# Moving the start addresses of two activation tiles in a two-layer decoder kernel

## The chip, the cores and the metric

The kernel runs on one core of a Trainium2 chip. The metric is the device time of one execution in microseconds. Three runs of the kernel before gave 1098.22, 1100.28 and 1100.70 us, so its median is 1100.28 us.

## The reference, cut to what matters

Two residual layers over 512 tokens of width 1024, in float32. Every layer is a mixer and then an MLP, each behind an RMS norm:

```
for i in range(2):
    h = rmsnorm(x, norm_mix[i])
    x = x + (mix_even(h, ...) if i % 2 == 0 else mix_odd(h, ...))
    h = rmsnorm(x, norm_mlp[i])
    x = x + mlp(h, w1[i], w2[i])

def mlp(h, w1, w2):              # w1: 1024 x 4096, w2: 4096 x 1024
    a = relu(h @ w1)
    return (a * a) @ w2
```

`mix_even` projects h and runs gated linear attention beside block-sparse softmax attention; `mix_odd` projects h and runs a short gated convolution beside a pooling mixer. Both end in a 1024 x 1024 output projection.

## The kernel before, in words

Activations lie transposed, features on the 128 partitions and the 512 tokens along the free dimension. Every large matrix product is done in three passes of a split type: an operand is kept as a rounded part `hi` and a remainder `lo`, and `mm3` (lines 126 to 129) issues hi x hi, hi x lo and lo x hi into one PSUM accumulation. So each 128 x 128 weight slice costs three matmuls of 512 columns (lines 127, 128, 129), each with its own load of 128 weight columns into TensorE (LDWEIGHTS).

Weights stream in as 184 blocks of 128 x 1024 float32. `block_parts` (lines 100 to 114) issues the DMA of a block into `raw` on SP's queue, ScalarE rounds it into `whi` (line 111) and VectorE subtracts it into `wlo` (line 112); two blocks are prepared ahead. A block feeds 24 matmuls of 512 columns.

The moving operand of these matmuls, the one that streams its columns past the loaded weights, is nearly always the tile `A`: 32 rows of 512 float32, that is 32 x 2048 bytes per partition. Rows 0 to 7 and 8 to 15 hold `hi` and `lo` of the normed layer input, rows 16 to 23 and 24 to 31 those of a mixer's output or of a group of the MLP's inner activations. The token projections (`tok_g`) use it the other way round, with `A` as weights and the weight block as moving operand.

The MLP works on four groups of 1024 inner features: `m1(g)` makes group g, `m2(g)` multiplies it by w2 and adds to x. Groups 0 and 2 lie in rows 16 to 31 of `A`, groups 1 and 3 in the tile `E`, 16 rows of 2048 bytes. The order is m1(0), m1(1), m2(0), m1(2), m2(1), m1(3), m2(2), m2(3), in program order on TensorE. The very last product of the kernel (`last_unit`) does half of its columns in pieces of 256.

Where the tiles lie: a pool's tiles follow each other in each partition in multiples of 32 bytes, and the pools follow each other. `A` is the last tile of pool `cp`; behind it come `wp` (raw, whi, wlo), `np` (norm helpers `ss`, `nt`, `rs`), and then the pools of the stage at hand, among them `E` and, in the odd mixer, `pwh`, `pwl` and `ph`. Before the change `A` starts at byte 40,896 of a partition, `raw` at 106,432, the first `whi` at 114,624, `E` at 155,584. What is left of these starts on division by 256 is the same, 192, and since rows are 2048 bytes and weight slices 512 bytes long, every row of `A` and `E` and every weight slice of `whi` and `wlo` starts on remainder 192 as well. Tiles with another remainder are rare: `ph` (pooling input, moving in lines 127 to 129 under the name pm, with `pwh` and `pwl` at 192 as weights) and `th` (softmax weights, moving in line 690, with `A` at 192 as weights) both start on remainder 0. `ones_r` (192, the weights of the norm sums nps, lines 275 and 276) and `kk` lie ahead of `A`.

Of the kernel before, what the change touches and what calls it, by code (L numbers as in the profile page):

```python
# [8 lines left out]
F32R = mybir.dt.float32r  # L9
# [5 lines left out]
P = 128  # L15
S = 512
# [28 lines left out]
def kernel(  # L45
# [14 lines left out]
    cp = ctx.enter_context(tc.tile_pool(name="cp", bufs=1))  # L60
# [16 lines left out]
    warm = cp.tile([P, 64], F32, name="warm")  # L77
    dve.memset(warm, 0.0)
    kk = cp.tile([P, KT, S], F32R, tag="x", name="kk")
    A = cp.tile([P, 32, S], F32R, name="A")  # L80
    ident = cn[:, C_ID : C_ID + P]
    ones = cn[:, C_ONE : C_ONE + P]
    dist = cn[:, C_DIST : C_DIST + S]
# [4 lines left out]
    def col(i, n=1):  # L88
        return vc[:, i : i + n]

    def mm_tile(name):
        return ps.tile([P, 2, S], F32, tag="mm", name=name, bufs=2)

    def m_tile(name, tag="tp"):
        return ps.tile([P, S], F32, tag=tag, name=name, bufs=2 if tag == "s" else 1)
# [23 lines left out]
    def wblock():  # L119
        while len(ready) < AHEAD + 1 and wcount[0] < w.shape[0]:  # L120
            emit_block()
        return ready.pop(0)

    def mm3(o, w_hi, w_lo, a_hi, a_lo, start, stop, swap=False):
        if swap:
            w_hi, w_lo, a_hi, a_lo = a_hi, a_lo, w_hi, w_lo
        pe.matmul(o, w_hi, a_hi, start=start, stop=False)  # L127
        pe.matmul(o, w_hi, a_lo, start=False, stop=False)  # L128
        pe.matmul(o, w_lo, a_hi, start=False, stop=stop)  # L129

    def t_unit_g(name, acts):
        o = mm_tile(name)
        n = len(acts)
        for b in range(n // 4):
# [3 lines left out]
            for kk in range(4):  # L138
                k = b * 4 + kk
                for j in range(2):  # L140
                    c = slice(j * P, (j + 1) * P)
                    mm3(o[:, j, :], hi[:, kk, c], lo[:, kk, c], A[:, acts[k][0], :], A[:, acts[k][1], :],
                        k == 0, k == n - 1)
# [11 lines left out]
    def t_unit(name, acts):  # L155
        return drain(t_unit_g(name, acts))

    def tok_g(name, evac):
        blocks = []
        for half in range(2):  # L160
            o = mm_tile(f"{name}{half}")
            for k in range(KT):
# [4 lines left out]
                for j in range(2):  # L167
                    t = slice((2 * half + j) * P, (2 * half + j + 1) * P)
                    mm3(o[:, j, :], hi[:, c], lo[:, c], A[:, k, t], A[:, 8 + k, t], k == 0, k == KT - 1, swap=True)
                if k == KT - 1:  # L170
# [84 lines left out]
    def split_h(k, gcol, src, c=slice(0, S)):  # L255
        act.activation(A[:, k, c], src[:, k, c], AF.Copy, scale=col(gcol + k))
        dve.scalar_tensor_tensor(  # L257
            A[:, 8 + k, c], src[:, k, c], col(gcol + k), A[:, k, c].bitcast(F32), op0=ALU.mult, op1=ALU.subtract
        )
# [23 lines left out]
    def bc2(t):  # L283
        return t[:, None, :].to_broadcast([P, 2, S])

    def x_add(o, n):
        dve.tensor_add(x[:, 2 * n : 2 * n + 2, :], x[:, 2 * n : 2 * n + 2, :], o)  # L287
# [13 lines left out]
    def mlp(l, nrm, nxt):  # L301
        with ExitStack() as c2:
            mp = c2.enter_context(tc.tile_pool(name=f"mp{l}", bufs=2, reuse_waits="tile"))
            E = mp.tile([P, 16, S], F32R, tag="E", name=f"E{l}", bufs=1)
            st = {}

            def aslot(f):
                i = f % 8
                if (f // 8) % 2 == 0:
                    return A[:, 16 + i, :], A[:, 24 + i, :]  # L310
                return E[:, i, :], E[:, 8 + i, :]

            def apair(f):
                i = f % 8
                if (f // 8) % 2 == 0:
                    return A[:, 16 + i : 18 + i, :], A[:, 24 + i : 26 + i, :]
                return E[:, i : i + 2, :], E[:, 8 + i : 10 + i, :]

            def m1(g):
                for q in range(4):  # L320
                    f = 8 * g + 2 * q
                    o = t_unit(f"m1_{l}_{f}", H)
                    if "rs" not in st:
                        st["rs"] = nrm.rs()
                    r = mp.tile([P, 2, S], F32, tag="r", name=f"r_{l}_{f}")
                    dve.scalar_tensor_tensor(r, o, 0.0, bc2(st["rs"]), op0=ALU.max, op1=ALU.mult)  # L326
                    act.activation(r, r, AF.Square)  # L327
                    hi, lo = apair(f)
                    act.copy(hi, r)  # L329
                    dve.tensor_sub(lo, r, hi.bitcast(F32))  # L330

            def last_unit(g, n):
                ws = [[t.rearrange("p (k n) -> p k n", k=4) for t in wblock()] for _ in range(2)]
                for j, c0, c1 in ((0, 0, S), (1, 0, S // 2), (1, S // 2, S)):
                    c = slice(j * P, (j + 1) * P)
                    row = 2 * n + j
                    o = m_tile(f"m2_{l}_{g}_{n}_{j}_{c0}", "tp" if c0 else "s")
                    for k in range(8):
                        hi, lo = ws[k // 4]
                        ah, al = aslot(8 * g + k)  # L340
                        mm3(o[:, c0:c1], hi[:, k % 4, c], lo[:, k % 4, c], ah[:, c0:c1], al[:, c0:c1], k == 0, k == 7)
                    dve.tensor_add(x[:, row, c0:c1], x[:, row, c0:c1], o[:, c0:c1])
                    nc.sync.dma_start(out[row * P : (row + 1) * P, c0:c1], x[:, row, c0:c1])

            def m2(g):
                for n in range(4):
                    if nxt is None and g == 3 and n == 3:
                        last_unit(g, n)
                        return
                    o = mm_tile(f"m2_{l}_{g}_{n}")  # L350
                    for b in range(2):
                        hi, lo = wblock()
                        hi = hi.rearrange("p (k n) -> p k n", k=4)
                        lo = lo.rearrange("p (k n) -> p k n", k=4)
                        for kk in range(4):
                            k = 4 * b + kk
                            ah, al = aslot(8 * g + k)
                            for j in range(2):
                                c = slice(j * P, (j + 1) * P)
                                mm3(o[:, j, :], hi[:, kk, c], lo[:, kk, c], ah, al, k == 0, k == 7)  # L360
                    x_add(o, n)
                    if g == 3:
                        for k in (2 * n, 2 * n + 1):
                            if nxt is not None:
                                nxt.step(k)
                            else:
                                nc.sync.dma_start(out[k * P : (k + 1) * P, :], x[:, k, :])

            m1(0)
            m1(1)  # L370
            m2(0)
            m1(2)
            m2(1)
            m1(3)
            m2(2)
            m2(3)
# [547 lines left out]
    even_mixer(n0, n1)  # L924
    n2 = Norm("n2", V_MIX + 8)
    mlp(0, n1, n2)
    n3 = Norm("n3", V_MLP + 8)
    odd_mixer(n2, n3)
    mlp(1, n3, None)


# [122 lines left out]
```

## Time and profile before

| | |
|---|---|
| median of three runs | 1100.28 us |
| profiled execution | 1100.57 us |
| its span, first to last instruction | 1098.8 us |
| PE busy | 1087.6 us, 99% of the span |
| DVE, ACT, POOL busy | 556.4, 405.4, 103.2 us |
| granted TensorE clock, mean | 0.998 |

A matmul's duration in the trace covers its whole passage through the array, and matmuls overlap; what one costs in a stream is the distance from its start to the start of the next, called its gap below.

### The profile page before, as it was taken

Reading aid. Unit: us, or ns where it says so; the run is one execution under the profiler, and the core shown is the slowest. Engines: PE = TensorE matmul, PEld = TensorE weight load, DVE = VectorE, ACT = ScalarE, POOL = GpSimd, SP = SyncE. Lnnn points to the kernel's source line nnn. Section 1 sums busy time; section 2 is a strip of 40 time slices with the busy share of each in tenths; the row PEclk is TensorE's granted clock in tenths of the full one; section 3 lists DMA queues with packets and bytes.
Section 4 is the critical chain, followed back from the end, with each engine's and each line's share of the span. In section 5 each row is a group of like instructions: output and inputs, shape, how many; then the busy total and the mean of one; then the engine's idle time right before and its main releaser. Section 6 shows DMA issues by size and latency. Waiting matters only on the chain.

```text
span 1098.8 us, 12567 instructions
## 1 busy us (share of the span) xinstructions
PE 1087.6 (99%) x5008; PEld 889.5 (81%) x5008; DVE 556.4 (51%) x774; ACT 405.4 (37%) x554; POOL 103.2 (9%) x110
## 2 busy tenths in 40 slices
PE   9999999999999999999999999999999999999998
PEld 6677778778888888888888888888888888888887
DVE  6887766767534334334334675455444344334331
ACT  6465555545434223224214332244433133133110
POOL 2132322314000000000001200021000000000000
PEclk9999999999999999999999999999999999999999
DMA  7223114122332322223322332323232223222231
GB/s 229 77 77 96 58 39 154 42 69 84 115 96 96 96 96 96 95 96 96 96 96 96 106 96 96 96 96 96 96 96 96 96 96 96 96 96 96 96 115 58
DMA packets 32043, 104.84 MB, mean 95 GB/s; under 512 B 3729, under 2 KB 6258, under 8 KB 31986
## 3 DMA queue, kind: packets, MB, share of 16 engines
q1 hardware_dynamic: 31202, 101.69, 28.5%
q0 software_dynamic: 640, 2.10, 0.6%
q8 instruction: 39, 0.64, 0.2%
q10 hardware_dynamic: 144, 0.26, 0.1%
q14 instruction: 18, 0.15, 0.0%
HBM read 101.94 MB, written 2.10 MB: 95 GB/s over the span
## 4 chain that ended last, share of the span: by engine, by line
PE 92%; DVE 4%; ACT 1%; DMA 1%; POOL 1%; issue 1%; SPq 0%; DVEq 0%; POOLq 0%
PE m L129 21%; PE m L128 21%; PE m L127 21%; PE wo L129 1%; PE wo L128 1%; PE wo L127 1%; DMA raw<-in_w_dram 1%; PE av L690 1%; PE s L642 1%; PE ptp L671 1%; PE s L641 1%; PE va L127 1%; PE va L129 1%; PE va L128 1%; PE xc L129 1%
## 5 line engine op out<-in xcount | busy, mean ns | idle before, releaser
L111 ACT CAST whi<-raw 128x1024 fp32r<-128x1024 f32 (+1 forms) x188 | 194.4, 1035 | 537.5 <-PE m L128 432.0
L112 DVE TENSOR_TENSOR wlo<-raw,whi 128x1024 fp32r<-128x1024 f32 (+1 forms) x188 | 228.1, 1214 | 201.4 <-ACT whi L111 201.2
L127 PE MATMUL m<-A,whi 128*128 128x512 f32 x768 | 298.8, 389 | 0.0
L128 PE MATMUL m<-A,whi 128*128 128x512 f32 x768 | 298.8, 389 | 0.0
L129 PE MATMUL m<-A,wlo 128*128 128x512 f32 x768 | 298.8, 389 | 0.0
L128 PEld LDWEIGHTS m<-A,whi 128*128 128x128 f32 x768 | 144.2, 188 | 30.1
L127 PEld LDWEIGHTS m<-A,whi 128*128 128x128 f32 x768 | 144.2, 188 | 29.8
L129 PEld LDWEIGHTS m<-A,wlo 128*128 128x128 f32 x768 | 144.2, 188 | 29.7
L128 PE MATMUL m<-E,whi 128*128 128x512 f32 (+1 forms) x264 | 101.0, 383 | 0.0
L129 PE MATMUL m<-E,wlo 128*128 128x512 f32 (+1 forms) x264 | 101.0, 383 | 0.0
L127 PE MATMUL m<-E,whi 128*128 128x512 f32 (+1 forms) x264 | 101.0, 383 | 0.0
L287 DVE TENSOR_TENSOR x<-x,m 128x1024 f32<-128x1024 f32 x31 | 37.9, 1221 | 109.1 <-PE m L129 109.1
L326 DVE SCALAR_TENSOR_TENSOR r<-m,rs_n 128x1024 f32<-128x1024 f32 x32 | 39.2, 1225 | 96.8 <-PE m L129 96.7
L268 POOL TENSOR_TENSOR ss_n<-ss_n,sq_n 128x512 f32<-128x512 f32 x21 | 32.8, 1562 | 391.7 <-ACT sq_n L266 391.0
L127 PEld LDWEIGHTS m<-E,whi 128*128 128x128 f32 x264 | 49.6, 188 | 9.8
L128 PEld LDWEIGHTS m<-E,whi 128*128 128x128 f32 x264 | 49.6, 188 | 9.7
L129 PEld LDWEIGHTS m<-E,wlo 128*128 128x128 f32 x264 | 49.6, 188 | 9.5
L327 ACT ACTIVATE r<-r 128x1024 f32<-128x1024 f32 x32 | 34.0, 1061 | 19.9 <-DVE r L326 19.9
L330 DVE TENSOR_TENSOR E<-r,E 128x1024 fp32r<-128x1024 f32 x16 | 19.6, 1225 | 17.2 <-ACT E L329 17.2
L257 DVE SCALAR_TENSOR_TENSOR A<-x,vc,A 128x512 fp32r<-128x512 f32 x24 | 27.3, 1141 | 1.2
L330 DVE TENSOR_TENSOR A<-r,A 128x1024 fp32r<-128x1024 f32 x16 | 19.6, 1225 | 15.1 <-ACT A L329 15.1
L127 PE MATMUL wo<-A,whi 128*128 128x512 f32 x64 | 24.9, 389 | 0.0
(297 smaller groups left out, 1414.3 us busy)
## 6 DMA issues: line engine op xcount, KB each, us to landing
raw<-in_w_dram SPq DMA_DIRECT2D x180, 512.0 KB, 3.3
xin<-in_xT_dram SPq DMA_DIRECT2D x16, 128.0 KB, 3.9
raw<-in_w_dram SPq DMA_DIRECT2D x8, 256.0 KB, 4.3
x<-in_xT_dram POOLq DMA_DIRECT2D x8, 256.0 KB, 4.9
out_dram<-x SPq DMA_DIRECT2D x7, 256.0 KB, 2.0
cn<-in_con_dram SPq DMA_DIRECT2D x1, 736.0 KB, 6.7
pw<-in_poolw_dram ACTq DMA_DIRECT2D x1, 256.0 KB, 2.7
out_dram<-x SPq DMA_DIRECT2D x2, 128.0 KB, 1.7
```

Source lines behind the costliest of these rows:

```text
L111: act.copy(hi[:, c], raw[:, c])
L112: dve.tensor_sub(lo[:, c], raw[:, c], hi[:, c].bitcast(F32))
L127: pe.matmul(o, w_hi, a_hi, start=start, stop=False)
L128: pe.matmul(o, w_hi, a_lo, start=False, stop=False)
L129: pe.matmul(o, w_lo, a_hi, start=False, stop=stop)
L257: dve.scalar_tensor_tensor(A[:, 8 + k, c], src[:, k, c], col(gcol + k), A[:, k, c].bitcast(F32), op0=ALU.mult, op1=ALU.subtract)
L268: (dve if first else pool).tensor_add(ss, ss, sq)
L287: dve.tensor_add(x[:, 2 * n : 2 * n + 2, :], x[:, 2 * n : 2 * n + 2, :], o)
L326: dve.scalar_tensor_tensor(r, o, 0.0, bc2(st["rs"]), op0=ALU.max, op1=ALU.mult)
L327: act.activation(r, r, AF.Square)
L330: dve.tensor_sub(lo, r, hi.bitcast(F32))
L641: pe.matmul(s_[:, :m], qs, kS[p][hh][:, :m], start=True, stop=False)
```

## The change

`A` is allocated 64 bytes longer, and the kernel uses it from byte 64 on. As everything behind `A` in the partition follows it, the weight tiles, the norm helpers and all later pools move by 64 bytes too. `E` is allocated 192 bytes longer and is used from byte 128 on in layer 0 and from byte 192 on in layer 1; the tiles behind `E` in its pool (`r`) move by these 192 bytes on top. No instruction is added, removed or reordered.

```diff
-    A = cp.tile([P, 32, S], F32R, name="A")
+    A = cp.tile([P, 32 * S + 16], F32R, name="A")[:, 16:].rearrange("p (k s) -> p k s", s=S)
...
-            E = mp.tile([P, 16, S], F32R, tag="E", name=f"E{l}", bufs=1)
+            e0 = (32, 48)[l]
+            E = mp.tile([P, 16 * S + 48], F32R, tag="E", name=f"E{l}", bufs=1)[:, e0 : e0 + 16 * S]
+            E = E.rearrange("p (k s) -> p k s", s=S)
```

Remainders of the starts on division by 256 bytes:

| tile | before | after |
|---|---|---|
| `A` | 192 | 0 |
| `whi`, `wlo`, `raw` | 192 | 0 |
| `E`, layer 0 / layer 1 | 192 / 192 | 128 / 192 |
| norm helpers `nt` | 192 | 0 |
| `ones_r`, `kk` | 192 | 192 |
| `ph` with `pwh` as weights | 0 with 192 | 64 with 0 |
| `th` with `A` as weights | 0 with 192 | 64 with 0 |

## Rows read from the trace of the kernel before

**Rows 1.** The page: span, part 1, the clock of part 2, part 4.

```profile
span 1098.8 us, 12567 instructions
PE 1087.6 (99%) x5008; PEld 889.5 (81%) x5008; DVE 556.4 (51%) x774; ACT 405.4 (37%) x554; POOL 103.2 (9%) x110
PEclk9999999999999999999999999999999999999999
PE 92%; DVE 4%; ACT 1%; DMA 1%; POOL 1%; issue 1%; SPq 0%; DVEq 0%; POOLq 0%
```

**Rows 2.** Instruction groups by shape, PE: line, names, tile, count | busy us, mean ns.

```profile
L127 PE MATMUL m<-A,whi 128*128 128x512 f32 x768 | 298.8, 389 | 0.0
...
L127 PE MATMUL m<-E,whi 128*128 128x512 f32 x248 | 96.5, 389 | 0.0
```

**Rows 3.** Timeline of PE (start us, us), two rows 192 matmuls apart, moving operand A.

```profile
318.59 0.39 PE L127 MATMUL m<-A,whi 128*128 128x512 f32 x1
...
362.11 0.39 PE L127 MATMUL m<-A,whi 128*128 128x512 f32 x1
```

**Rows 4.** Timeline of PE, the 192 matmuls on E of m2(1), layer 0.

```profile
438.27 0.39 PE L127 MATMUL m<-E,whi 128*128 128x512 f32 x1
...
481.79 0.39 PE L127 MATMUL m<-A,whi 128*128 128x512 f32 x1
```

**Rows 5.** Stretches: us, busy by engine, then PEclk (granted clock), DMA, GB/s.

```profile
33.00:34.80 1.80, 1.80 (x5) 1.36 (x5) 1.01 (x7) 0.52 (x2) 0.00 (x0) 0.50 0.81 198
276.00:317.00 41.00, 41.00 (x182) 33.97 (x181) 20.99 (x19) 16.47 (x17) 0.00 (x0) 1.00 0.30 97
```

**Rows 6.** Timeline of PE in the first of these stretches.

```profile
33.14 0.63 PE L127 MATMUL kb<-whi,A 128*128 128x512 f32 x1
...
33.99 0.63 PE L129 MATMUL kb<-whi,A 128*128 128x512 f32 x1
```

**Rows 7.** Timeline of PE around pm, whose moving operand starts on another remainder.

```profile
645.44 0.40 PE L127 MATMUL pm<-ph,pwh 128*128 128x512 f32 x1
645.68 0.40 PE L128 MATMUL pm<-ph,pwh 128*128 128x512 f32 x1
...
646.83 0.40 PE L127 MATMUL xc<-A,whi 128*128 128x512 f32 x1
...
649.15 0.39 PE L128 MATMUL xc<-A,whi 128*128 128x512 f32 x1
```

**Rows 8.** Timeline of PE around the norm sums nps.

```profile
274.62 0.39 PE L275 MATMUL nps_n<-ss_n,ones_r 128*128 128x512 f32 x1
274.85 0.39 PE L276 MATMUL nps_n<-ss_n,ones_r 128*128 128x512 f32 x1
...
275.98 0.39 PE L128 MATMUL m<-A,whi 128*128 128x512 f32 x1
```

**Rows 9.** Matmuls of 256 columns by line: duration ns min/median/max, first and last start.

```profile
L127 PE MATMUL m<-E,whi x12: 283/283/283, 1090.5 to 1094.5; 128*128 128x256 f32 x12
...
L690 PE MATMUL av<-th,A x3: 278/279/280, 145.7 to 145.9; 128*128 128x256 f32 x3
```

**Rows 10.** Timeline of PE, 46 gaps of 256 columns on E.

```profile
1089.53 0.28 PE L128 MATMUL m<-E,whi 128*128 128x256 f32 x1
...
1095.05 0.28 PE L129 MATMUL m<-E,wlo 128*128 128x256 f32 x1
```

**Rows 11.** VectorE by line, 1024 elements, operands on different remainders: ns min/median/max.

```profile
L326 DVE SCALAR_TENSOR_TENSOR r<-m,rs_n x32: 1224/1225/1225, 279.1 to 1008.0; 128x1024 f32<-128x1024 f32 x32
...
L899 DVE TENSOR_TENSOR cg<-cg,rs x2: 1223/1224/1225, 645.6 to 679.7; 128x1024 f32<-128x1024 f32 x2
```

**Rows 12.** Waits: who for whom, us in total, times, longest.

```profile
ACT whi L111 <- PE m L128: 432.0, 119, 4.4
...
ACT whi L111 <- DMA raw<-in_w_dram: 12.0, 9, 4.3
```

## The prediction

> **What bounds the kernel now.** I read the page first. PE is busy 99% of a span of 1098.8 us at a granted clock whose mean is 0.9 or more in each of the 40 slices, and the chain that ended last lies on PE for 92% of the span [rows 1]. So time is decided by the gap from one matmul's start to the next, and by little else. Next the groups by shape: on each of the lines 127 to 129, 768 matmuls of 512 columns stream rows of A and 248 stream rows of E in the MLPs, all with a mean duration of 389 ns and no idle time before them [rows 2]. Durations overlap, so I went to the timeline. 192 matmuls on A take 362.11 - 318.59 = 43.52 us, a gap of 226.7 ns [rows 3]; 192 on E take 481.79 - 438.27 = 43.52 us, the same gap [rows 4].
>
> Is 226.7 ns the least that 512 columns can cost? The early stretch says no. At a granted clock of 0.50, the lower level of 1.2 GHz, against 1.00 later on [rows 5], two gaps take 33.99 - 33.14 = 0.85 us, 425 ns each, which is one column per cycle (512/1.2 = 426.7) with nothing on top [rows 6]. One column per cycle at 2.4 GHz would be 213.3 ns. At full clock each matmul therefore pays 13.3 ns, or 32 cycles, that it doesn't pay at half the clock. A fixed cost per instruction would not vanish at the lower clock; two streams of reads that get in each other's way at the full rate could. The two streams would be the moving row and the weight slice of the next matmul, which is loaded beside it. The 256-column matmuls on E agree: 46 gaps take 1095.05 - 1089.53 = 5.52 us, 120.0 ns each, and 256/2.4 = 106.7, so again 13.3 ns more [rows 10]. In all these rows both streams start on the same remainder modulo 256 bytes.
>
> Do remainders matter at all? Two places let me look. pm streams `ph` (remainder 0) against weights at 192. The regular gap ends with its first matmul: 0.24 us to the second [rows 7]. From pm's start to the xc matmul at 649.15 there are 16 gaps in 3.71 us, 231.9 ns each; only then is the gap 226.7 again. nps is a change of tiles too, with weights and moving both at 192, and its gaps stay regular: from 274.62 to 275.98 six gaps take 1.36 us, 226.7 ns each [rows 8]. So a difference of remainders between moving and weights disturbs the stream, not a change of tile. The second place is av, `th` at 0 against weights at 192: its 256-column matmuls last 278 to 280 ns where those on E last 283 [rows 9]. Duration less gap is 389 - 227 = 162 for 512 columns [rows 2, 3] and 283 - 120 = 163 for 256, so av's gaps are some 3 to 5 ns shorter than E's.
>
> **The change, part by part.** No instruction is added, removed or moved, no semaphore or queue changes.
>
> 1. A and all behind it move by 64 bytes. The 184 blocks x 24 matmuls are 4,416; less the 744 on E (3 x 248) and less 24 that the last product replaces by 48 of 256 columns, 3,648 stream A against weights or weights against A. Both sides move alike, so the difference of remainders stays 0. I cost this at nothing. Nothing in the trace shows all tiles moved together, so the bounds are 5.2 ns to either side (the 231.9 of [rows 7] less 226.7), 19 us each way; I keep that as a rival, since the nearest row, a stream with equal remainders, keeps its gap whichever row or slice is used [rows 3, 4].
>
> 2. E against its weights: the difference becomes 128 bytes in layer 0 and 192 in layer 1, for 744 matmuls of 512 columns and 48 of 256. Not shown before, so bounded by rows. Below: no interference, 213.3 ns, so 744 x 13.3 = 9.9 us less, and 48 x 13.3 = 0.6 us less. Above: the unsettled stream of pm and xc, 744 x 5.2 = 3.9 us more, and 0.2 us more for the 48. Of the two rows with a difference, pm's is six matmuls after a break and runs on into xc, where the difference is 0 again, so it shows the break and not what an unequal stream settles at; av is the one that recurs with its own gap, and it is 3 to 5 ns shorter. I take 5 ns a matmul, above a third of the 13.3: 744 x 5 + 48 x 3 = 3.9 us less.
>
> 3. Breaks. E starts and ends four times, and each passage may cost what pm's did: 3.71 - 16 x 0.2267 = 0.08 us. Eight times is 0.6 us at most; as pm's 0.08 holds two breaks (into pm, out of it), 0.3 us. nps now has a difference (192 for `ones_r`, 0 for `nt`) in the three places that are in steady stream: 0.2 us. Together 0.5 us more. The attention matmuls that mix A with `kk`, 32 of them, could move by 13 ns at most, 0.4 us either way; I count none.
>
> 4. VectorE, ScalarE, the DMAs. A 1024-element operation takes 1225 ns on tiles at 192 and 1224 on `cg`, which starts on remainder 0 [rows 11], so their prices stay. What hides them: ScalarE waits 432.0 us in total for TensorE before it rounds the next weights, and 12.0 us for the DMA [rows 12]. If PE gains 4 us over the four stretches on E, some 180 us long, this cover, up to 4.4 us a block, is still there, and nothing else comes late.
>
> Sum: 0 - 3.9 + 0.5 = 3.4 us less than the profiled execution's 1100.57 us (its span and 1.8 us around it), 1097.2 us. That execution is 0.3 us over the median, so against the median 1096.9; I say 1097.0.
>
> The Trainium skill puts a bare figure on the gap: "TensorE: Matmul & The Clock Gate", section "Back-to-back issue gap", gives N/2.4 + 2.5 ns for a warm isolated one, 215.8 ns for 512 columns. By it, E freed of all interference would give an estimated 744 x 10.9 = 8.1 us, and the time would be about 1093; the trace before shows no 512-column gap that short in a steady stream.
>
> **Rivals.**
>
> (a) E settles at the old gap. A disturbed stream finds its way back to 226.7 (as xc does 10 matmuls after pm), whatever the difference. For it: the two lengths, 512 and 256 columns, pay exactly the same 13.3 ns; against it: av. Then only the breaks are left: 1100.6 + 0.5, against the median 1100.8 us.
> The Trainium skill speaks for this one: "SBUF — State Buffer", section "A bandwidth-pool intuition that's wrong", gives LDWEIGHTS a second, independent read port, so the streams could not meet and no address would matter; the irregular gaps behind pm speak against a rule that strict.
>
> (b) Slower: E never settles. The regular gap is a state that needs equal remainders, and E's 744 matmuls run like the 16 of pm and xc. Its place is the four stretches on E, its price 3.9 + 0.2 us, with the breaks 4.6 us more: 1104.9 us. It decides from a gap of 226.7 on: every ns above it is 0.74 us. For it: pm shows nothing settling in six matmuls; against it: xc was just as irregular with equal remainders, and av is regular and shorter.
>
> (c) The start itself counts, not the difference: with A and the weights on remainder 0 all 3,648 matmuls change. At 5.2 ns that is 19 us: 1081 or 1119. Against it: pm's moving operand starts on 0 and is not quicker for it.
>
> (d) The addresses don't move as the diff says, because the space behind A is laid out anew; then E alone would differ, and the time is that of the forecast, (a) or (b).
>
> **How the numbers follow.** Forecast 0.44, reaching from 1090 (nothing left of the 13.3 ns, breaks added) to 1099 (2 ns gained); (a) 0.29, 1100 to 1101.5; (b) 0.20, 1102 to 1105; (c) 0.07, of which 0.04 down and 0.03 up; (d) is spread over the others. Range for 8 in 10: 1090 to 1105; that leaves out (c) and the edges of the forecast and of (b). What a measurement of this kernel can tell from no change is about 0.2%, 2.2 us: below 1098.1 faster, above 1102.5 slower. Faster: 0.42 of the forecast's 0.44 and 0.04 of (c), 0.46. Slower: 0.19 of (b) and 0.03 of (c), 0.22. The rest, 0.32, is the same.
>
> **What would show it.** Step 1: 192 matmuls on A still take 43.52 us. Step 2: the 192 on E take 42.6 us (gap 221.7); 43.5 would be rival (a), 44.5 rival (b). Layer 0 and layer 1 need not agree, since 128 and 192 bytes differ. Step 3: irregular gaps for some ten matmuls behind each change between A and E and behind nps. Step 4: the same durations on VectorE and ScalarE, and ScalarE still waiting for TensorE and not for the DMA. The prediction is wrong at its root if the gap on A moves.

## The result: slower, 1106.57 us for 1099.59

Four runs each: 1106.57 us (1105.02 to 1107.53) with the change, 1099.59 us (1098.22 to 1100.70) before, a ratio of 1.0063 with a 95% interval of [1.0045, 1.0081]. The profiled execution took 1107.12 us, 6.55 more than that of before.

The page of the kernel after, the lines that answer to [rows 1]: the span, the busy times, the clock in 40 slices, the chain.

```profile
span 1105.3 us, 12567 instructions
PE 1093.2 (99%) x5008; PEld 890.8 (81%) x5008; DVE 556.2 (50%) x774; ACT 405.5 (37%) x554; POOL 102.6 (9%) x110
PEclk9899999999999999999999999999999999999999
PE 92%; DVE 3%; ACT 1%; DMA 1%; POOL 1%; issue 1%; SPq 0%; POOLq 0%; DVEq 0%
```

The same instructions, the same engines busy for the same time, except PE. So to the timeline of PE after: a stretch of 192 matmuls on A, answering [rows 3], then m2(1) on E in layer 0, answering [rows 4], and m2(1) on E in layer 1 (start us, us).

```profile
320.36 0.39 PE L127 MATMUL m<-A,whi 128*128 128x512 f32 x1
...
363.88 0.39 PE L127 MATMUL m<-A,whi 128*128 128x512 f32 x1
...
440.04 0.40 PE L127 MATMUL m<-E,whi 128*128 128x512 f32 x1
...
484.83 0.39 PE L127 MATMUL m<-A,whi 128*128 128x512 f32 x1
...
925.17 0.39 PE L127 MATMUL m<-E,whi 128*128 128x512 f32 x1
...
969.97 0.39 PE L127 MATMUL m<-A,whi 128*128 128x512 f32 x1
```

A: 363.88 - 320.36 = 43.52 us, as before, a gap of 226.7 ns. E: 44.79 and 44.80 us, gaps of 233.3 ns, 6.7 ns or 16 cycles longer, in both layers; in layer 1 every gap lies between 232 and 235 ns, in layer 0 they alternate between some 229 and 238 about the same mean. The other two E stretches do the same (44.79 us for 192 and 39.20 for 168; before 43.52 and 38.08). Together the four lost 4.9 us.

One thing on E became faster. The 256-column matmuls at the very end, which answer [rows 10]:

```profile
1096.35 0.28 PE L128 MATMUL m<-E,whi 128*128 128x256 f32 x1
...
1101.57 0.28 PE L129 MATMUL m<-E,wlo 128*128 128x256 f32 x1
```

46 gaps in 5.22 us, 113.5 ns each, where before they took 120.0: 0.3 us won. VectorE and the wait for the DMA are as they were; these rows answer to [rows 11, 12] (duration min/median/max, and waits).

```profile
L328 DVE SCALAR_TENSOR_TENSOR r<-m,rs_n x32: 1223/1225/1225, 280.8 to 1013.7; 128x1024 f32<-128x1024 f32 x32
...
L901 DVE TENSOR_TENSOR cg<-cg,rs x2: 1223/1224/1224, 650.0 to 684.1; 128x1024 f32<-128x1024 f32 x2
```

```profile
ACT whi L111 <- PE m L128: 436.5, 119, 4.6
...
ACT whi L111 <- DMA raw<-in_w_dram: 12.2, 9, 4.3
```

That makes 4.9 - 0.3, and some 0.1 for the breaks (a stretch on A behind an E stretch or behind nps takes 43.53 to 43.54 us instead of 43.52). The rest of the 6.55 us arises ahead of E: its first matmul starts at 440.04 us after and at 438.27 before. Whether these 1.8 us belong to the change is the first thing to ask.

### The profile page after: what moved, and what is told of

Its sections match the earlier page's. It is cut to its first block, busy times and chain, and to the rows that moved or that the text cites. A ratio compares the mean times of both kernels' runs of the same rounds, so it can differ in the third digit from the quotient of the medians.

```text
span 1105.3 us, 12567 instructions
## 1 busy us (share of the span) xinstructions
PE 1093.2 (99%) x5008; PEld 890.8 (81%) x5008; DVE 556.2 (50%) x774; ACT 405.5 (37%) x554; POOL 102.6 (9%) x110
## 4 chain that ended last, share of the span: by engine, by line
PE 92%; DVE 3%; ACT 1%; DMA 1%; POOL 1%; issue 1%; SPq 0%; POOLq 0%; DVEq 0%
PE m L128 21%; PE m L129 21%; PE m L127 21%; PE wo L129 1%; PE wo L127 1%; PE wo L128 1%; PE av L692 1%; DMA raw<-in_w_dram 1%; PE s L644 1%; PE ptp L673 1%; PE s L643 1%; PE va L127 1%; PE va L129 1%; PE va L128 1%; PE xc L127 1%
## 5 line engine op out<-in xcount | busy, mean ns | idle before, releaser
L127 PE MATMUL m<-E,whi 128*128 128x512 f32 (+1 forms) x264 | 102.4, 388 | 0.0
L128 PE MATMUL m<-E,whi 128*128 128x512 f32 (+1 forms) x264 | 102.3, 388 | 0.0
L328 DVE SCALAR_TENSOR_TENSOR r<-m,rs_n 128x1024 f32<-128x1024 f32 x32 | 39.2, 1224 | 96.9 <-PE m L129 96.8
L332 DVE TENSOR_TENSOR A<-r,A 128x1024 fp32r<-128x1024 f32 x16 | 19.6, 1224 | 15.1 <-ACT A L331 15.1
```

## The experiments

Theory D: what counts is the difference between the start of the moving row and the start of the weight slice, modulo 256 bytes. Its rivals: the start itself (S), and a cost in the first 60 us (C).

**Each part alone.** `a_alone` has the first hunk of the diff only, `e_alone` the second only.

```diff
 a_alone
+    A = cp.tile([P, 32 * S + 16], F32R, name="A")[:, 16:].rearrange("p (k s) -> p k s", s=S)
 e_alone
+            e0 = (32, 48)[l]
+            E = mp.tile([P, 16 * S + 48], F32R, tag="E", name=f"E{l}", bufs=1)[:, e0 : e0 + 16 * S]
```

> The first part of the change alone: A, the weight tiles and all behind them 64 bytes later, E on the same remainder as the weights again. Theory D (the gap is set by the difference of the starts of moving row and weight slice modulo 256 bytes; equal starts 226.7 ns, those of E in the change 233.3): every E stretch of 192 matmuls back to 43.5 us, all of A at 43.5 us, so the time of before within 0.2%, plus whatever the first 62 us add. Theory S (the start itself counts, or anything that moves with the 64 bytes): the time goes up by part of the 6.5 us here, most of it outside E. Theory C (1.6 us of the change's 6.5 us lie in the first 60 us and come from the 64 bytes): about 1.6 us slower than before, all of it before 62 us.

> The second part alone: E 128 and 192 bytes later in the two layers, A and the weights where they were. Theory D: the same differences as in the change, so each E stretch takes 44.8 us and the time rises by about 5.1 us (4 x 1.27), 0.46%. Theory S: E now starts on remainder 64 in layer 0 and 128 in layer 1, other starts than in the change; the stretches need not take 44.8 us, and layer 0 and layer 1 would change places at best. Theory C: none of the 1.6 us in the first 62 us.

`a_alone`: 1100.49 us against 1100.09, ratio 1.000 [0.9989, 1.0012]. `e_alone`: 1105.10 us, ratio 1.0042 [1.0026, 1.0058]. Timeline of `a_alone`, m2(1) of layer 0:

```profile
438.51 0.39 PE L127 MATMUL m<-E,whi 128*128 128x512 f32 x1
...
482.03 0.39 PE L127 MATMUL m<-A,whi 128*128 128x512 f32 x1
```

and of `e_alone`, m2(1) of both layers:

```profile
439.37 0.40 PE L127 MATMUL m<-E,whi 128*128 128x512 f32 x1
...
484.16 0.39 PE L127 MATMUL m<-A,whi 128*128 128x512 f32 x1
...
924.45 0.39 PE L127 MATMUL m<-E,whi 128*128 128x512 f32 x1
...
969.25 0.39 PE L127 MATMUL m<-A,whi 128*128 128x512 f32 x1
```

43.52 us where all moved together; 44.79 and 44.80 where E moved against the weights, the very times of the change, though E now starts on remainders 64 and 128 instead of 128 and 192. The differences, 128 and 192, are what the two kernels share. S falls. C falls too: E's first matmul comes at 438.51 us in `a_alone`, with the 64 bytes, and at 439.37 in `e_alone`, without them.

**The change once more**, unaltered, in six runs.

> The change once more, unaltered, for a tighter ratio. Theory D (only E's difference to the weights costs): 4 stretches x 1.27 us, so 0.46%, like E moved alone (0.42% measured); the 1.6 us that the change's first profile lost before 62 us were chance and are not there in the median. If the two parts add something together: over 0.6% again, and A's stretches or the first 62 us show where.

1105.31 us against 1100.43, ratio 1.0051 [1.0033, 1.0068]. Its first matmul on E starts at 437.8 us, earlier than before's; in the other runs of this study that leave A at its gap, that start lies anywhere from 435.9 to 439.5. So the 1.8 us of the first profile don't belong to the change. They go with the clock that TensorE was granted: here are the stretches from 20 to 40 us of the kernel before and of the first profile after (us, busy by engine, granted clock, DMA, GB/s).

```profile
20.00:40.00 20.00, 17.96 (x79) 12.50 (x78) 15.99 (x32) 10.76 (x19) 4.20 (x4) 0.91 0.41 130
...
20.00:40.00 20.00, 16.90 (x69) 11.91 (x69) 13.57 (x28) 9.27 (x18) 3.67 (x4) 0.83 0.40 132
```

0.91 before and 0.83 after; 0.08 of 20 us is 1.6 us. The mean granted clock of a whole run varies from 0.997 to 1.0 over the runs, and the time goes with it (the kernel before: 1102.6 us at 0.997, 1098.9 at 1.0, medians); why it varies the runs don't show. At one and the same mean clock, 0.998, the change took 1105.11 us (median of 5 runs) and the kernel before 1100.45 (of 14): 4.7 us. What the traces account for, 4.9 - 0.3 + 0.1 = 4.7 us or 0.43%, is just that; it lies inside this run's interval and that of E alone, and just under the first one's lower end of 0.45%.

**The weights moved instead.** In `w_moved` A stays and all behind it goes 64 bytes later.

```diff
+    A = cp.tile([P, 32 * S + 16], F32R, name="A")[:, : 32 * S].rearrange("p (k s) -> p k s", s=S)
```

> A stays where it was and the weight tiles, with E and all else behind A, go 64 bytes later: E's difference to the weights is 0 again, A's becomes 192 (64 in the token projections, where A is the weights). Theory D, with the weights as the partner: every A stretch of 192 goes from 43.5 to 44.8 us, E's stay at 43.5; 3,264 matmuls x 6.67 ns and 384 x 2.3 ns make 22.7 us, about 1122 us. If the partner were anything else (A's other rows, the stores of the other engines into E): A's stretches stay at 43.5 us and the time at 1100 us.

1120.81 us against 1100.43, ratio 1.0189 [1.0171, 1.0207]; 20.4 us more by the medians where 22.7 were expected. Timeline of `w_moved`: a stretch on A, and m2(1) on E.

```profile
319.41 0.40 PE L127 MATMUL m<-A,whi 128*128 128x512 f32 x1
...
364.21 0.40 PE L127 MATMUL m<-A,whi 128*128 128x512 f32 x1
...
442.61 0.39 PE L127 MATMUL m<-E,whi 128*128 128x512 f32 x1
...
486.17 0.39 PE L127 MATMUL m<-A,whi 128*128 128x512 f32 x1
```

Now A, which did not move, takes 44.80 us, and E, which moved with the weights, 43.56 (0.04 of it a break). The partner of the moving row lies behind A, and the weights are what TensorE reads there. What is missing of the 22.7 us lies ahead of the first MLP: from its first matmul on the span grew by 19.2 us, just what the 2,880 matmuls on A that stand there cost at 6.67 ns each. The stores of other engines and of the DMA into the moved tiles are a rival, but in m2(1) of layer 1 after the change, where every gap is long, VectorE and ScalarE work in only 15.55 and 10.43 of 44.70 us and the DMA engines in 30% of it, so their stores don't explain it (the view of [rows 5]):

```profile
925.20:969.90 44.70, 44.70 (x193) 35.90 (x192) 15.55 (x13) 10.43 (x10) 0.00 (x0) 1.00 0.30 95
```

**The differences, four to a run.** E got an offset of its own in m2(1) and m2(3) of each layer.

```diff
+            EO = ((16, 24), (40, 56))[l]
+            Et = mp.tile([P, 16 * S + 56], F32R, tag="E", name=f"E{l}", bufs=1)
+            Eg = [Et[:, e : e + 16 * S].rearrange("p (k s) -> p k s", s=S) for e in EO]
...
+                E = Eg[f // 16]
```

> E of the kernel before, moved by 64 bytes in m2(1) and 96 in m2(3) of layer 0, and by 160 and 224 in layer 1: four differences to the weights in one run. Theory D with steps of 64 bytes: 64 as 192 (233.3 ns), 96, 160 and 224 somewhere between 226.7 and 233.3. Theory B (only a difference of 0 modulo 64 bytes keeps a stream regular): 96, 160 and 224 are worse than 233.3, some 240 ns. The forecast's idea that some difference lets the streams pass each other: one of the four is under 224 ns (a stretch under 43.0 us).

> The same with 32 and 256 bytes in layer 0, 16 and 384 in layer 1. Theory D modulo 256: 256 gives 226.7 ns and 43.5 us like no offset; 384 gives what 128 gave in the change, 233.3 ns and 44.8 us. If the period is longer than 256 bytes, 256 is slow too. 16 and 32 bytes tell how fine the grain is: 226.7 if addresses count in units of 64 bytes, else another gap.

> E moved by 240 and 8 bytes in layer 0, by 48 and 208 in layer 1. Seen so far: 0 and 256 give 226.7 ns, 16 gives 231.7, 64 gives 229.0, 32, 96, 128, 192 and 224 give 233.3, 160 gives 234.3. Theory D with collisions between the two reads of 16 cycles (6.7 ns) each, two where starts are equal and three elsewhere: 8 and 240 (16 short of a whole period) lie between 226.7 and 232, 48 and 208 at 233. A gap under 226.0 ns at any of the four would show that the start of before is not the best one, and 744 matmuls at, say, 220 ns would win 5 us.

> E moved by 80 and 112 bytes in layer 0, by 144 and 248 in layer 1. Theory D as above: 80 near the 229 of 64 or on the way to the 233.4 of 96, 112 and 144 at 233 to 234, 248 (8 short of a whole period) near 227 to 230. Anything under 226.0 ns is a better start than before.

Gap of the 512-column matmuls, from the length of each stretch over its 192 matmuls (168 in m2(3) of layer 1):

| difference, bytes | gap, ns | difference | gap | difference | gap |
|---|---|---|---|---|---|
| 0 | 226.7 | 80 | 231.1 | 192 | 233.3 |
| 8 | 232.5 | 96 | 233.4 | 208 | 234.7 |
| 16 | 231.7 | 112 | 231.1 | 224 | 233.3 |
| 32 | 233.3 | 128 | 233.3 | 240 | 233.3 |
| 48 | 233.3 | 144 | 233.3 | 248 | 232.2 |
| 64 | 229.0 | 160 | 234.3 | 256 / 384 | 226.7 / 233.3 |

Three of the readings on which the table rests, in the timelines of `scan2` (256 bytes), `scan1` (64) and `scan3` (240):

```profile
570.45 0.39 PE L127 MATMUL m<-E,whi 128*128 128x512 f32 x1
...
613.97 0.39 PE L127 MATMUL u<-A,whi 128*128 128x512 f32 x1
```

```profile
435.93 0.40 PE L127 MATMUL m<-E,whi 128*128 128x512 f32 x1
...
479.90 0.40 PE L127 MATMUL m<-A,whi 128*128 128x512 f32 x1
```

```profile
435.93 0.40 PE L127 MATMUL m<-E,whi 128*128 128x512 f32 x1
...
480.73 0.39 PE L127 MATMUL m<-A,whi 128*128 128x512 f32 x1
```

43.52, 43.97 and 44.80 us. A whole period of 256 bytes costs nothing and 384 costs what 128 does. The expectations missed 8 and 240, which were to lie between 226.7 and 232, 64 (233.3 expected), 112 (233 to 234) and 248 (227 to 230); 80 does lie between 64 and 96. The values at 64, 80 and 112 follow no order that I named. Above all, none of the differences tried beats 0, so no version came out of this that is faster than the kernel before. The single times of the four kernels, 1102.57, 1104.25, 1103.32 and 1105.78 us, all lie above the medians of before, 1100.09 and 1100.43; the evidence is the stretches, since single runs of the kernel before reach 1103.57.

**Only one of the two parts of a product moved.** `lo_moved` shifts the tiles wlo alone; `e_lo` leaves the weights and shifts only half of E's rows, in the last stretch the lo rows by 128 bytes.

```diff
 lo_moved
+        lo = wp.tile([P, 1024 + 64], F32R, tag="wlo", name=f"wlo{i}")[:, 16 : 16 + 1024]
 e_lo
+            EO = (((0, 48), (0, 16)), ((48, 0), (0, 32)))[l]      # offsets of the hi and lo rows
```

> Only the remainder tiles wlo start 64 bytes later than in the kernel before; A, E and whi keep equal starts. In each triple of matmuls the weights of line 129 are wlo, and they are loaded while line 128 streams. Theory N (a row collides with the slice that is loaded beside it, the next matmul's): the gap from line 128's start to line 129's grows, towards 233 ns or beyond, and the other two stay near 226.7; a triple takes some 687 ns for 680, a stretch of 192 matmuls 43.9 us, the kernel about 1110. Theory O (a row collides with its own weights in some way): line 129's gap grows instead. Theory P (the loads have nothing to do with it, and w_moved's cost came from whi alone): no gap grows and the time is 1100 us.

> The weights stay; of E only one half moves, so only one kind of row has an unequal start. Layer 0: the lo rows, by 192 bytes in m2(1) and 64 in m2(3). Layer 1: the hi rows by 192 in m2(1), the lo rows by 128 in m2(3). lo rows stream in line 128 alone, hi rows in 127 and 129. When wlo alone was moved, the gap of line 129 grew most (235.8 ns; 229.1 and 228.4 in 128 and 127), though the trace puts the load of wlo beside line 128. Theory O (a row collides with its own weights): with moved lo rows the gap of line 128 grows most. Theory N2 (a row collides with the slice loaded beside it, and the recorded starts run one matmul ahead of the stream): line 129 grows most again, since the moved row of line 128 meets the load of wlo there. Either way about 13 ns a triple for 192 bytes, as wlo alone did, 44.4 us a stretch; moved hi rows the like or up to the 20 ns a triple that moving both costs, 44.8 us.

`lo_moved` took 1117.79 us for 1100.16 in one run, not the 1110 expected: each stretch of 192 takes 44.37 us, 693 ns a triple for 680. As wlo alone moved, the weights are shown to be a partner. `e_lo` took 1102.61 for 1100.97, one run each, at mean clocks of 1.0 and 0.998. Its stretches came to 43.96 us (lo by 192; 44.4 expected), 44.53 (lo by 64), 44.99 (hi by 192; 44.8 at most expected) and, for lo by 128, 38.45 for 168. Here is first where `lo_moved` records the load of wlo, then the durations by line (min/median/max ns) in `lo_moved`, 321 to 365 us, and in `e_lo`, 1060 to 1085 us (lo by 128); a longer gap to the next matmul shows as a longer duration, since duration less gap is 162 ns.

```profile
330.88 0.39 PE L128 MATMUL m<-A,whi 128*128 128x512 f32 x1
330.88 0.19 PEld L129 LDWEIGHTS m<-A,wlo 128*128 128x128 f32 x1
```

```profile
L127 PE MATMUL m<-A,whi x64: 388/390/390, 320.9 to 364.6; 128*128 128x512 f32 x64
...
L128 PE MATMUL m<-A,whi x64: 391/392/393, 321.2 to 364.8; 128*128 128x512 f32 x64
...
L129 PE MATMUL m<-A,wlo x64: 397/398/398, 320.7 to 364.4; 128*128 128x512 f32 x64
```

```profile
L127 PE MATMUL m<-E,whi x37: 389/389/389, 1060.0 to 1084.7; 128*128 128x512 f32 x37
...
L128 PE MATMUL m<-E,whi x37: 395/395/395, 1060.2 to 1084.9; 128*128 128x512 f32 x37
...
L129 PE MATMUL m<-E,wlo x37: 388/388/388, 1059.7 to 1084.5; 128*128 128x512 f32 x37
```

With wlo moved, line 129 grows most, the matmul that uses wlo, and not line 128, beside which the load of wlo is recorded: theory N falls as it was put. With the lo rows moved by 128, line 128 alone grows, the matmul that streams them: theory N2 falls in that stretch. Both fit theory O, by which the price appears at the matmul whose own row and own weights start unequally. But the other stretches don't. With lo by 192 the surplus spreads over all three lines (gaps of 229.0, 229.3 and 228.3 ns). With hi by 192 (`e_lo`, 922 to 965 us), line 128 grows most, and it streams lo rows against whi, both unmoved:

```profile
L127 PE MATMUL m<-E,whi x62: 397/398/398, 921.7 to 964.6; 128*128 128x512 f32 x62
...
L128 PE MATMUL m<-E,whi x62: 397/399/400, 922.0 to 964.8; 128*128 128x512 f32 x62
...
L129 PE MATMUL m<-E,wlo x61: 388/388/397, 922.2 to 964.4; 128*128 128x512 f32 x61
```

And a difference that all three lines share can show unevenly too, as in `scan4` at 112 bytes (572 to 614 us), where the gaps are 231, 237 and 225 ns:

```profile
L127 PE MATMUL m<-E,whi x61: 392/392/392, 572.3 to 613.9; 128*128 128x512 f32 x61
...
L128 PE MATMUL m<-E,whi x61: 398/398/398, 571.8 to 613.4; 128*128 128x512 f32 x61
...
L129 PE MATMUL m<-E,wlo x61: 387/387/388, 572.1 to 613.7; 128*128 128x512 f32 x61
```

So the line on which a surplus shows doesn't tell which reads meet, and theory O is not shown either. What these two runs show is that moving the weights of one matmul in three, or half of the rows, is enough to cost time. Which read waits for which inside the engine stays open.

## Why the prediction was wrong

**What bounds the kernel** held: gap times number is the time. The 13.3 ns over one column per cycle are still there in every stream with equal starts. That they are interference, because a fixed cost would not vanish at the lower clock, was an inference from two rows; nothing here bears it out, and where they come from stays open.

**Step 1**, A and the weights moving together: right. 43.52 us, and 1.000 for that part alone. So rival (c) falls. That gap can't decide rival (d), since it would be the same had nothing moved. The break behind nps can, whose weights `ones_r` lie ahead of A: the 720 matmuls on A behind it take 163.22 us in `a_alone` and in the change, and 163.20 in `e_alone` and before, so the norm helpers behind A did move.

**Step 2** failed, and it is nearly the whole error. It priced E's 744 matmuls at 5 ns less, arguing that "av is the one that recurs with its own gap, and it is 3 to 5 ns shorter". They cost 6.7 ns more: 744 x 11.7 = 8.7 us between forecast and fact, 1097.0 + 8.7 = 1105.7. The row av was read rightly and carried over wrongly. It has 256 columns, and for 256 columns an unequal start does save time: 120.0 became 113.5 ns on E's own last matmuls, at a difference of 192 bytes. For 512 columns the same difference has the other sign. At other differences those matmuls gain less: at 128 bytes (384 in `scan2`) 118.7 ns, and at 208, 224 and 248 between 118.2 and 119.8. A single row, of three matmuls of another length and at another difference (`th` on 0 against 192 is 64 bytes, not 128 or 192), was allowed to decide a sign. The row of the right length was pm, also at 64 bytes, and I set it aside as a break.

The idea behind step 2 was that equal starts are where the two streams collide, and that moving one of them could only help. The scan says the reverse for 512 columns: 0 is the best of the 17 differences modulo 256 that were tried, and 226.7 ns was not a price of equal starts but the lowest gap among them. The price that all share, 13.3 ns, is not removed by any offset tried.

**Rival (b)** named the right place, E's four stretches, and the right sign, and said when it decides. Its mechanism was half right: the stream does settle, but to another gap, 233.3 instead of 226.7, and not to the unsettled 231.9 of pm. So its price was 5.2 where 6.7 was measured, and its 1104.9 us came close to 1105.3 and 1106.6 partly by luck: pm's difference is 64 bytes, at which E later settled at 229.0. I gave it 0.20, and it should have stood first. The range ended at 1105, short of the first result: the upper bound was taken from pm's 16 gaps, of which ten have equal starts again and are on their way back.

The Trainium skill speaks of this in "SBUF — State Buffer", section "A bandwidth-pool intuition that's wrong", which gives LDWEIGHTS a second read port independent of the moving operand's. Rival (a) read into it that the two streams can't meet and that no address matters; `w_moved` lost 20.4 us by 64 bytes, so the measurement decides against that reading. How many ports there are the runs don't show.

**Step 3**, the breaks: right in kind, too large. They were priced at 0.5 us together and cost some 0.1; a stretch behind a break is about 0.02 us longer in the change, and 0.05 at most in the other runs.

**Step 4**, everything but PE: right, 1225 and 1224 ns, 12.2 us of waiting for the DMA.

## What to carry to other kernels

Where TensorE is the bound and streams rows of 512 columns against weights without a pause, as in the float32r matmuls here, look at the starts of both tiles modulo 256 bytes, and keep them equal: a harmless-looking pad between an activation tile and the weight tiles cost 1.9% here. Measure the gap over a stretch of a hundred or more matmuls, where 0.1 ns can be seen and the kernel's own noise can't reach. And before a row is carried over, ask whether it has the same shape: here 256 and 512 columns gave opposite signs.

## What the runs showed that I had not expected

Many of the settled gaps lie a multiple of 16 cycles of 2.4 GHz apart. One matmul of 512 columns takes 544 cycles with equal starts and 560 at eight of the other sixteen differences (226.7, 233.3 ns); one of 256 takes 288 with equal starts and 272 at 192 bytes (120.0, 113.5 ns; 272 cycles are 113.3). Over a triple of matmuls, 64 bytes cost about 16 cycles more than equal starts, 80 and 112 cost 32, and 32, 48, 96, 128, 144, 192, 224 and 240 cost 48; 8, 16, 160, 208 and 248 don't fit (36 to 58). Eight bytes are enough to leave the good state (232.5 ns). And where a difference was measured in several places, it gave the same gap in each: 128 bytes gave 233.3 ns in the change, in the repeat, in E alone and as 384, and 192 gave 233.3 in E and, by moving the weights, in A.
